# Modulation blocks in the array's quarters, filter directions on its row halves, and weight blocks loaded earlier

## The chip, the cores and the metric

The kernel runs on one core of one Trainium2 chip. A core has a matrix unit (TensorE, in the profile PE, with its weight loads as PEld), VectorE (DVE), ScalarE (ACT), GpSimd (POOL) and SyncE (SP), which here issues the DMA transfers. They work from their own queues, each in its own order, and wait for one another by semaphores. The metric is the device time of one execution in microseconds; less is better.

## The reference, cut to what matters

Two layers of a hybrid diffusion trunk run on 128 context tokens and 1024 latent tokens with the same weights. Each layer is RMSNorm, a shift and scale, a mixer, a gate, and a residual add; shift, scale and gate come from a conditioning vector (the "modulation").

```python
def ada_mod(cvec, w, b):
    m = jax.nn.silu(cvec) @ w + b
    shift, scale, gate = jnp.split(m, 3, axis=-1)
    return shift[:, None], scale[:, None], gate[:, None]
```

For layer l, w has shape (1024, 3072), and there are two conditioning vectors: one for the context, one for the latents. Layer 0's mixer has SSD heads and Hyena channels side by side, behind one projection of 1024 to 6688 columns; layer 1's is a neighbourhood attention. A Hyena channel is a long convolution whose filter comes from a small network of the token's position, once forward and once backward:

```python
    hdn = jnp.sin(freq * (feats @ w1 + b1))
    hdn = jnp.sin(freq * (hdn @ w2 + b2))
    filt = (hdn @ w3).astype(f32)
    decay = jnp.exp(-t * jnp.abs(deltas)[None])
    h_fwd = filt[:, :D_B] * decay
    h_bwd = filt[:, D_B:] * decay
```

The last step is `y = rms_norm(x + g * out)` on both streams.

## The kernel before, in words

Activations lie transposed: 128 of the 1024 features on the partitions, all 1152 tokens along the row, so eight tiles make one activation. Precise products are split in three: a tile or a weight block is cut into a high part (a cast by ScalarE, line 132 for weights) and the rest (a subtraction by VectorE, line 133), and TensorE does high x high, high x low and low x high. A projection (`proj`, lines 160 to 162) takes one block of weights of 1024 x 128, loops over three blocks of 384 tokens and eight feature tiles, and so issues 72 products. Weight blocks come in a fixed list; `w_next` splits the next one and loads the one after.

Beside these projections runs background work. `self.bg` is a list of generators; after each block of 384 tokens `tick` adds a rate to a credit and takes as many steps of the first generator as there is credit. The order in which the instructions then stand on each engine isn't that of the source: a planner lays it out from the dependencies, the order of the source as priority, and its own estimates of time. Tiles come from pools; tiles of one tag share as many buffers as the pool has, and a new one waits until the old one's last reader is done. PSUM, where products are summed, has two pools: three banks for projections (`pj`) and five for all else (`ps`, in the profile bg).

What the change touches, in the order of time:

- **Start** (`run`, from line 1413 on). x is loaded in eight tiles on SP's queue (at the end of `open`'s small loads and the filter network's), then the modulation blocks 0 and 1, the first weight block, modulation block 2, the second weight block, and more modulation blocks. ScalarE squares x, VectorE adds the eight squares (line 1484), TensorE sums them over the features (`token_sums`, line 347), and `rstd_rep` makes the norm factors of them: a power on GpSimd, three diagonal blocks on VectorE, three products (line 338), copies. `make_h` then makes the eight modulated tiles (lines 355 to 361), in step with the first two projections. In between, the filter network is fed step by step: `filter_mlp` yields after each piece, and `sin_layer` is its sine: five operations of VectorE and one of ScalarE, with a scratch tile `k` (tag "sq" in the start's own pool). The squares use the buffers hh6, hh7 and hh0 of the later activation in turn; the last one is in hh6.
- **Filters** (`filter_groups` and `filter_time`, in the background of the stage "xbc", rate 1.0). For each of eight groups of 128 channels `filter_time` makes the filter in time: nine blocks of 128 positions, three products each (lines 514 to 516), whose weights are the network's 128 rows (64 forward, 64 backward) and whose moving side is w3, laid out as a block-diagonal matrix of 128 x 256 with zeros written by GpSimd. Two blocks share a bank; ScalarE makes four decays (line 519, tile dc) and VectorE multiplies them in (line 520). Then come a Fourier stage on VectorE and TensorE and a store of the spectrum.
- **Modulation** (`ada_gen`, `ada_mm`, `ada_row`, `ada_cols`, in the background of the stage "z", rate 2.0). Sixteen blocks of 256 columns. For each, four products at a time stand side by side in the array's columns, 32 each (line 290): they take four different blocks of 128 rows of the weights, in two halves. So a bank holds four partial sums in four quarters of its partitions; a row copy takes it out (line 296), and two selecting products (line 306) add the four quarters up and turn the result to columns, to which VectorE adds the bias (line 309). For the last gate the rows go to DRAM (growd).
- **Final stage** (`final`). The gate of layer 1 is needed along the row here: growd's 128 rows are loaded, and four selecting products (line 1364) with the constant sel4b spread the sum to all partitions; VectorE adds the bias (line 1365). They stand behind the fifth of eight steps of the first six output blocks.

Of the kernel before, what the change touches and what calls it, by code (L numbers as in the profile page):

```python
# [9 lines left out]
AF = mybir.ActivationFunctionType  # L10
# [7 lines left out]
T = 1152  # L18
# [29 lines left out]
class Net:  # L48
# [147 lines left out]
    def open(self):  # L196
# [18 lines left out]
        self.sel4 = self.t(self.p_c, [128, 2], "sel4")  # L215
        self.dma(self.sel4, i["sel4"])
        d = self.p_d
        self.Hd = self.t(d, [8, 128, 20, 128], "Hd")
# [8 lines left out]
        self.x1d = self.t(d, [NCH, 128, 1024], "x1d")  # L227
        self.growd = self.t(d, [128, 1024], "growd")
        self.Cd = self.t(d, [3, 16, 16, 480], "Cd")
# [20 lines left out]

    def ada_gen(self, blocks, pool):

        self.silu_wide(pool)
        todo = [(l, nb, half) for l, nb in blocks for half in range(2)]
        raw = {}

        def load(i):
            if i < len(todo):
                raw[i] = self.t(pool, [128, 1024], "wa", bufs=6)
                l, nb, half = todo[i]  # L260
                self.dma(raw[i], self.i["wada"][l, nb, half])

        for i in range(4):
            load(i)
        yield
        last = None
        for i, (l, nb) in enumerate(blocks):
            load(2 * i + 4)
            load(2 * i + 5)
            p = self.ps()  # L270
            self.ada_mm(p, 0, raw.pop(2 * i))
            yield
            self.ada_mm(p, 1, raw.pop(2 * i + 1))
            if last:
                self.ada_cols(*last)
            last = l, nb, self.ada_row(l, nb, p, pool)
            yield
        self.ada_cols(*last)

# [13 lines left out]
    def ada_row(self, l, nb, p, pool):  # L293

        row = self.t(pool, [128, 256], "row", bufs=2)
        self.nc.scalar.copy(row, p[:, :256])
        if l == 1 and nb >= 8:
            self.store(self.growd[:, (nb - 8) * 256:(nb - 7) * 256], row)
        return row
# [66 lines left out]

    def sin_layer(self, arg, pool):

        nc = self.nc
        M = 1.5 * 2.0 ** 23  # L370
        k = self.t(pool, [128, T], "sq")[:, 0:1152]
        nc.vector.tensor_scalar(out=k, in0=arg, scalar1=1.0 / (2 * math.pi), scalar2=M, op0=ALU.mult, op1=ALU.add)
        nc.vector.tensor_scalar(out=k, in0=k, scalar1=-M, scalar2=None, op0=ALU.add)
        nc.vector.scalar_tensor_tensor(out=arg, in0=k, scalar=-6.28125, in1=arg, op0=ALU.mult, op1=ALU.add)
        nc.vector.scalar_tensor_tensor(out=arg, in0=k, scalar=-(2 * math.pi - 6.28125), in1=arg, op0=ALU.mult, op1=ALU.add)
        nc.vector.tensor_scalar(out=arg, in0=arg, scalar1=3.1415925, scalar2=-3.1415925, op0=ALU.min, op1=ALU.max)
        nc.scalar.activation(arg, arg, AF.Sin)

    def filter_mlp(self, keep, pool, px):
# [18 lines left out]
        yield  # L398
        self.sin_layer(a, px)
        yield  # L400
# [8 lines left out]
        yield  # L409
        self.sin_layer(b, px)  # L410
        yield
# [76 lines left out]
    def filter_time(self, g, pool):  # L488

        nc = self.nc  # L490
        i = self.i

        w3 = self.t(pool, [128, 256], "w3")
        wh = self.t(pool, [128, 256], "w3h", F32R)
        wl = self.t(pool, [128, 256], "w3l", F32R)
        nc.gpsimd.memset(w3[0:64, 128:256], 0.0)
        nc.gpsimd.memset(w3[64:128, 0:128], 0.0)
        for h in range(2):
            self.dma(w3[64 * h:64 * h + 64, 128 * h:128 * h + 128], i["hw3"][:, g, h])
# [3 lines left out]
        self.dma(dl.rearrange("p a c -> p (a c)"), i["dlhb"][g:g + 1].to_broadcast([128, 256]))  # L503
        F = self.t(pool, [128, 18, 128], "F", bufs=2)
        Fj = F[:, 0:16].rearrange("p (d j) c -> p j d c", d=2)
        hh, hl = self.hdn
        for j0 in range(0, 9, 2):
            n = min(2, 9 - j0)
            p = self.ps()
            dc = self.t(pool, [128, 2, 2, 128], "dc")  # L510
            for j in range(j0, j0 + n):
                o = p[:, (j - j0) * 256:(j - j0) * 256 + 256]
                js = slice(j * 128, j * 128 + 128)
                nc.tensor.matmul(o, hh[:, js], wh, start=True, stop=False)
                nc.tensor.matmul(o, hl[:, js], wh, start=False, stop=False)
                nc.tensor.matmul(o, hh[:, js], wl, start=False, stop=True)
                for d in range(2):
                    n1 = 8 * d + j if j < 8 else 16 + d
                    nc.scalar.activation(dc[:, j - j0, d], dl[:, 0], AF.Exp, scale=self.tcol[:, n1:n1 + 1])
            nc.vector.tensor_tensor(out=Fj[:, j0:j0 + 2] if n == 2 else F[:, 16:18].unsqueeze(1),  # L520
                                    in0=p[:, :n * 256].rearrange("p (j d c) -> p j d c", j=n, d=2), in1=dc[:, :n], op=ALU.mult)

        nc.vector.tensor_tensor(out=F[0:1, 0:17:16], in0=F[0:1, 0:17:16], in1=bc(dl[0:1, 1:2], [1, 2, 128]), op=ALU.add)
        return F

    def filter_groups(self, pool):
# [4 lines left out]
        self.dma(self.tcol, self.i["tcol"])  # L531
        Fn = self.filter_time(0, pool)
        yield
        for g in range(8):
            F = Fn
            sm = self.t(pool, [128, 8, 128], "sm")
# [4 lines left out]
            yield  # L541
            if g < 7:
                Fn = self.filter_time(g + 1, pool)
                yield
            H = self.t(pool, [128, 20, 128], "H")
# [791 lines left out]
    def final(self, pool, ys, ws):  # L1337
# [19 lines left out]
        for k in range(8):  # L1357
            for (c, b), p in first.items():
                mm(p, c, slice(b * 512, b * 512 + 512), k)
            if k == 4:  # L1360
                for s in range(2):
                    for b in range(2):
                        p = self.ps()
                        nc.tensor.matmul(p, sel4b[:, s, :], rows[:, b * 512:(b + 1) * 512], start=True, stop=True)
                        V.tensor_tensor(out=gr[:, s, b * 512:(b + 1) * 512], in0=p, in1=bg[:, b * 512:(b + 1) * 512], op=ALU.add)
        for c in range(NCH):
# [46 lines left out]
    def run(self, upto="end"):  # L1413
# [21 lines left out]
        with self.pool("x0") as px:  # L1435
# [6 lines left out]
            def load(n):  # L1442
# [11 lines left out]
                for half in range(2):  # L1454
                    self.dma(r[half], self.i["wada"][0, blocks[n], half])
                raws[n] = r
# [198 lines left out]
def host(x):  # L1655
# [10 lines left out]

    o["wada"] = con(x["w_ada"].reshape(2, 2, 4, 128, 12, 256).transpose(0, 4, 1, 3, 2, 5).reshape(2, 12, 2, 128, 1024))

# [58 lines left out]
def constants():  # L1727
# [10 lines left out]
    o["sel4"] = s4.reshape(128, 2)  # L1738
    o["sel4b"] = np.ascontiguousarray(np.repeat(o["sel4"][:, :, None], 128, 2))
    o["sel64"] = np.tile(np.eye(32, dtype=f), (2, 1))  # L1740
# [101 lines left out]
```

## Time and profile before

| | |
|---|---|
| three runs, us | 2075.86, 2077.14, 2079.71 |
| profiled execution, us | 2079.07, its span 2077.3 |
| granted TensorE clock of the profiled execution | 0.995 |
| moved by DMA | 257.13 MB, mean 124 GB/s |
| filter products (lines 514, 515, 516) | 72 each, 287, 281 and 281 ns |
| modulation products (line 290), all stages | 19.8 us busy in the z stage, 256 records |
| selecting products (line 306), z stage | 64 records, 253 ns |

How to read it: an instruction on single-precision numbers stands as two records, one on numbers that are cut to fewer bits (fp32r) as one. Matmuls are pipelined: a product of 384 columns lasts some 340 ns in the records, but the next one starts 0.17 us after it. So a group's busy time or mean says little of what it costs TensorE, and the distance from start to start says more. The rows of the order of time give: start, length, engine, line, operation, written and read tiles, shape, count, and in brackets the idle time before and what ended it.

### The profile page before, as it was taken

How to read it: one execution, taken by the hardware profiler on the slowest of the kernel's cores; microseconds unless marked ns; L12 is line 12 of the kernel's file. 1: busy time of each engine (PE TensorE's matmuls, PEld its weight loads, DVE VectorE, ACT ScalarE, POOL GpSimd, SP SyncE). 2: the span in 40 equal slices, each digit the busy share in tenths (PEclk: the TensorE clock that was granted, in tenths of full speed). 3: DMA queues.
4: the chain of work that ended last, by engine and by line, in shares of the span. 5: the costliest groups of instructions: out<-in, count | busy, mean ns of one | idle time of the engine just before them, and what ended most of it. 6: DMA issues, size and time to landing. Idle time of an engine off the chain costs nothing.

```text
span 2077.3 us, 33946 instructions
## 1 busy us (share of the span) xinstructions
PE 2019.4 (97%) x13088; PEld 1820.7 (88%) x13088; DVE 1313.7 (63%) x2720; ACT 917.9 (44%) x2100; POOL 110.5 (5%) x233
## 2 busy tenths in 40 slices
PE   5999999999999999999999999999999999999998
PEld 3999997889999999888888899998888888888877
DVE  6887745145778787898899774654444344454464
ACT  3676642263333322554466511535445454443232
POOL 0010001110000000000000000100000000000000
PEclk9999999999999999999999999999999999999999
DMA  8142349554222113433353351422333223333462
GB/s 340 47 150 93 107 166 295 206 181 163 80 74 72 65 58 102 152 120 127 117 180 109 129 167 41 120 81 86 95 115 88 78 79 97 111 117 123 129 212 82
DMA packets 114265, 257.13 MB, mean 124 GB/s; under 512 B 27031, under 2 KB 62487, under 8 KB 111639
## 3 DMA queue, kind: packets, MB, share of 16 engines
q1 hardware_dynamic: 98728, 191.87, 29.1%
q0 software_dynamic: 15376, 63.09, 8.3%
q8 instruction: 104, 1.70, 0.4%
q14 instruction: 57, 0.47, 0.1%
HBM read 187.10 MB, written 67.80 MB: 123 GB/s over the span
## 4 chain that ended last, share of the span: by engine, by line
PE 82%; DVE 7%; DMA 4%; ACT 3%; issue 3%; SPq 0%; POOL 0%; POOLq 0%; DVEq 0%; ACTq 0%
PE pj L160 15%; PE pj L161 15%; PE pj L162 15%; PE bg L1315 3%; PE bg L1327 3%; PE bg L1298 3%; PE pj L1155 2%; PE pj L1156 2%; PE pj L1157 2%; PE bg L778 1%; PE bg L777 1%; PE bg L915 1%; PE pj L1353 1%; PE bg L290 1%; PE pj L1354 1%
## 5 line engine op out<-in xcount | busy, mean ns | idle before, releaser
L160 PE MATMUL pj<-hh,whi 128*128 128x384 f32 x1728 | 601.1, 348 | 2.7 <-DVE acc L846 1.8
L161 PE MATMUL pj<-hl,whi 128*128 128x384 f32 x1728 | 586.4, 339 | 0.0
L162 PE MATMUL pj<-hh,wlo 128*128 128x384 f32 x1728 | 586.1, 340 | 0.0
L160 PEld LDWEIGHTS pj<-hh,whi 128*128 128x128 f32 x1728 | 324.7, 188 | 23.7 <-issue 18.0
L161 PEld LDWEIGHTS pj<-hl,whi 128*128 128x128 f32 x1728 | 324.9, 188 | 7.5 <-issue 6.6
L162 PEld LDWEIGHTS pj<-hh,wlo 128*128 128x128 f32 x1728 | 324.6, 188 | 5.5 <-issue 4.5
L133 DVE TENSOR_TENSOR wlo<-wraw,whi 128x1024 fp32r<-128x1024 f32 x108 | 131.7, 1221 | 156.0 <-ACT whi L132 153.3
L132 ACT CAST whi<-wraw 128x1024 fp32r<-128x1024 f32 x108 | 113.3, 1050 | 259.1 <-PE pj L161 229.6
L1233 DVE CUSTOM_DVE_ANT_0 sz<-bg,Tb 128x512 f32<-128x512 f32 x128 | 83.5, 688 | 127.3 <-PE bg L1298 126.7
L583 ACT COPY raw<-pj 128x384 f32<-128x384 f32 (+2 forms) x140 | 56.0, 402 | 171.2 <-PE pj L162 84.0
L1235 ACT ACTIVATE sz<-sz,mx 128x512 f32<-128x512 f32 x128 | 91.6, 717 | 54.0 <-DVE mx L1233 53.2
L160 PE MATMUL pj<-yhi,whi 128*128 128x384 f32 x324 | 111.4, 344 | 3.8 <-DVE x L1076 2.8
L162 PE MATMUL pj<-yhi,wlo 128*128 128x384 f32 x324 | 110.8, 342 | 0.0
L161 PE MATMUL pj<-ylo,whi 128*128 128x384 f32 x324 | 109.7, 339 | 0.0
L1329 ACT COPY Pt<-bg 128x512 f32<-128x512 f32 (+1 forms) x144 | 71.9, 548 | 32.1 <-PE bg L1327 28.3
L1155 PE MATMUL pj<-whi,hh 128*128 128x256 f32 x288 | 82.9, 289 | 0.0
L1156 PE MATMUL pj<-wlo,hh 128*128 128x256 f32 x288 | 80.8, 281 | 0.0
L1157 PE MATMUL pj<-whi,hl 128*128 128x256 f32 x288 | 80.5, 280 | 0.0
L1327 PE MATMUL bg<-csq,sz 128*128 128x128 f32 x528 | 73.9, 280 | 0.0
L908 ACT ACTIVATE xw<-xt,wd 128x64 f32<-128x64 f32 x256 | 64.6, 336 | 8.7 <-PE bg L915 8.1
L1327 PEld LDWEIGHTS bg<-csq,sz 128*128 128x128 f32 x528 | 56.7, 141 | 13.0 <-issue 12.7
L160 PEld LDWEIGHTS pj<-yhi,whi 128*128 128x128 f32 x324 | 61.4, 189 | 7.1 <-issue 5.5
(411 smaller groups left out, 4021.3 us busy)
## 6 DMA issues: line engine op xcount, KB each, us to landing
wraw<-in_we SPq DMA_DIRECT2D x52, 512.0 KB, 3.6
wa<-in_wada SPq DMA_DIRECT2D x32, 512.0 KB, 6.8
wraw<-in_wo SPq DMA_DIRECT2D x24, 512.0 KB, 3.6
Tb<-Cd SPq DMA_DIRECT2D x256, 48.0 KB, 2.0
Hd<-H POOLq DMA_DIRECT2D x8, 1280.0 KB, 5.4
H<-Hd SPq DMA_DIRECT2D x8, 1280.0 KB, 6.5
xt<-xtd SPq DMA_DIRECT2D x17, 512.0 KB, 4.5
wraw<-in_woe SPq DMA_DIRECT2D x16, 512.0 KB, 4.2
```

Source lines behind the costliest of these rows:

```text
L132: self.nc.scalar.copy(hi, r)
L133: self.nc.vector.tensor_tensor(out=lo, in0=r, in1=hi.bitcast(F32), op=ALU.subtract)
L160: nc.tensor.matmul(p[:, :NB], wh, xh[k][:, sl], start=(k == 0), stop=False)
L161: nc.tensor.matmul(p[:, :NB], wh, xl[k][:, sl], start=False, stop=False)
L162: nc.tensor.matmul(p[:, :NB], wl, xh[k][:, sl], start=False, stop=(k == nk - 1))
L1155: nc.tensor.matmul(p[:, :256], self.hh[k][:, ts], hi[:, q:q + 256], start=(k == 0), stop=False)
L1156: nc.tensor.matmul(p[:, :256], self.hh[k][:, ts], lo[:, q:q + 256], start=False, stop=False)
L1157: nc.tensor.matmul(p[:, :256], self.hl[k][:, ts], hi[:, q:q + 256], start=False, stop=(k == 7))
L1233: V.tensor_tensor_reduce(out=z[:, :n], in0=s, in1=tb, scale=-1.0, scalar=3.0e38, op0=ALU.add, op1=ALU.min, accum_out=m1)
L1235: nc.scalar.activation(z[:, :n], z[:, :n], AF.Exp, bias=m1, scale=-1.0, accum_out=sm)
L1327: nc.tensor.transpose(pt[:, b * 128:(b + 1) * 128], p[:, b * 128:(b + 1) * 128], self.ident)
L1329: nc.scalar.copy(t[:, :nb * 128], pt[:, :nb * 128])
```

## The change

Four things are done.

1. *Start.* The first two weight blocks are loaded directly after x, ahead of all modulation blocks. The first sine layer takes its scratch from the buffer hh6, the second as before. A small constant (sel8) is loaded behind sel4.
2. *Filters.* `filter_time` makes two groups at a time. w3's two halves of 64 rows hold the forward and the backward weights of both groups side by side, without zeros; every product takes 64 rows, forward on the upper half of the array and backward on the lower, each into its own bank. The decays and the evacuation go by group and direction. It is called four times in place of eight, for the next pair behind the first part of the odd group's spectrum. The bias row hb takes w3's buffer.
3. *Modulation.* In the z stage four groups of 1024 columns take the place of sixteen blocks of 256. The four quarters of the array now hold the same block of 128 rows of the conditioning vectors, and each takes another 256 columns of the weights; eight steps add up in one bank. The result stands as it is, with no partial sums. Two selecting products with sel8 (8 columns) serve a whole group. The start's eight blocks stay as they were.
4. *Final stage.* growd is only 2 rows. They are loaded to all partitions, and VectorE adds the bias; the selecting products and sel4b go.

The diff, cut to its core:

```diff
-    def ada_gen(self, blocks, pool):
+    def ada_gen(self, groups, pool):
...
-        todo = [(l, nb, half) for l, nb in blocks for half in range(2)]
+        todo = [(n, k) for n in range(len(groups)) for k in range(8)]
...
+        def cols(l, a, row):
+            q = self.ps()
+            for j in range(2):
+                nc.tensor.matmul(q[:, 8 * j:8 * j + 8], row[:, j * 128:(j + 1) * 128], self.sel8, start=True, stop=True)
+            m = self.mod[l][0][:, a]
...
         last = None
-        for i, (l, nb) in enumerate(blocks):
-            load(2 * i + 4)
-            load(2 * i + 5)
-            p = self.ps()
-            self.ada_mm(p, 0, raw.pop(2 * i))
+        for i, (n, k) in enumerate(todo):
+            load(i + 4)
+            if k == 0:
+                p = self.ps()
+            w = raw.pop(i)
+            for b in range(4):
+                nc.tensor.matmul(p[32 * b:32 * b + 32, :256], self.cs[:, k, :], w[:, b * 256:(b + 1) * 256],
+                                 start=(k == 0), stop=(k == 7))
+            if k == 1 and last:
+                cols(*last)
+            if k == 7:
+                l, a = groups[n]
+                row = self.t(pool, [128, 256], "row", bufs=2)
+                nc.scalar.copy(row, p[:, :256])
+                if (l, a) == (1, 2):
+                    for b in range(4):
+                        self.store(self.growd[:, b * 256:(b + 1) * 256], row[32 * b:32 * b + 2, :])
+                last = l, a, row
             yield
...
-        self.sin_layer(a, px)
+
+        self.sin_layer(a, self.t(self.p_h, [128, T], "hh6")[:, 0:1152])
...
-        self.sin_layer(b, px)
+        self.sin_layer(b, self.t(px, [128, T], "sq")[:, 0:1152])
...
-        w3 = self.t(pool, [128, 256], "w3")
+        w3 = self.t(pool, [128, 2, 128], "w3")
...
-        nc.gpsimd.memset(w3[0:64, 128:256], 0.0)
-        nc.gpsimd.memset(w3[64:128, 0:128], 0.0)
         for h in range(2):
-            self.dma(w3[64 * h:64 * h + 64, 128 * h:128 * h + 128], i["hw3"][:, g, h])
+            self.dma(w3[64 * h:64 * h + 64], i["hw3"][:, g:g + 2, h])
...
+        hb = self.t(pool, [128, 2, 128], "w3")
+        for m in range(2):
+            self.dma(dl[:, m], i["dlhb"][g + m:g + m + 1, 0:128].to_broadcast([128, 128]))
+            self.dma(hb[0:1, m], i["dlhb"][g + m:g + m + 1, 128:256])
+        Fs = [self.t(pool, [128, 18, 128], "F", bufs=2) for n in range(2)]
...
+            ps = [self.ps(), self.ps()]
             for j in range(j0, j0 + n):
...
+                for x, w, st, sp in ((hh, wh, True, False), (hl, wh, False, False), (hh, wl, False, True)):
+                    for r, p in zip(R, ps):
+                        nc.tensor.matmul(p[:, o], x[r, js], w[r], start=st, stop=sp)
+            for m, F in enumerate(Fs):
+                dc = self.t(pool, [128, 2, 2, 128], "dc")
+                for d, p in enumerate(ps):
+                    n1 = 8 * d + j0 if j0 < 8 else 16 + d
+                    for j in range(n):
+                        nc.scalar.activation(dc[:, d, j], dl[:, m], AF.Exp, scale=self.tcol[:, n1 + j:n1 + j + 1])
+                    nc.vector.tensor_tensor(out=F[:, n1:n1 + n], in0=p[:, :n * 256].rearrange("p (j g c) -> p g j c", j=n, g=2)[:, m],
+                                            in1=dc[:, d, :n], op=ALU.mult)
...
-            if g < 7:
-                Fn = self.filter_time(g + 1, pool)
-                yield
...
+            if g in (1, 3, 5):
+                Fs = self.filter_time(g + 1, pool)
+                yield
...
-        sel4b = self.t(pool, [128, 2, 128], "sel4b", bufs=1)
-        self.dma(sel4b, self.i["sel4b"])
-        rows = self.t(pool, [128, 1024], "x1t")
-        self.dma(rows, self.growd)
+        for s in range(2):
+            self.dma(gr[:, s], self.growd[s:s + 1].to_broadcast([128, 1024]))
+            V.tensor_tensor(out=gr[:, s], in0=gr[:, s], in1=bg, op=ALU.add)
...
-            if k == 4:
-                for s in range(2):
-                    for b in range(2):
-                        p = self.ps()
-                        nc.tensor.matmul(p, sel4b[:, s, :], rows[:, b * 512:(b + 1) * 512], start=True, stop=True)
-                        V.tensor_tensor(out=gr[:, s, b * 512:(b + 1) * 512], in0=p, in1=bg[:, b * 512:(b + 1) * 512], op=ALU.add)
...
-            load(0)
-            load(1)
             self.w_load(0)
-            load(2)
             self.w_load(1)
-            for n in (3, 4, 5, 7):
+            for n in (0, 1, 2, 3, 4, 5, 7):
                 load(n)
...
-        self.bg.append(self.ada_gen([(0, nb) for nb in range(8, 12)] + [(1, nb) for nb in range(12)], p_ad))
+        self.bg.append(self.ada_gen([(0, 2), (1, 0), (1, 1), (1, 2)], p_ad))
```

More of the change, by code (lines that the diff above doesn't have):

```diff
@@ L216, in open @@
         self.dma(self.sel4, i["sel4"])
+        self.sel8 = self.t(self.p_c, [128, 8], "sel8")
+        self.dma(self.sel8, i["sel8"])
         d = self.p_d
@@ L227, in open @@
         self.x1d = self.t(d, [NCH, 128, 1024], "x1d")
[L228 removed]
+        self.growd = self.t(d, [2, 1024], "growd")
         self.Cd = self.t(d, [3, 16, 16, 480], "Cd")
@@ L259, in load @@
                 raw[i] = self.t(pool, [128, 1024], "wa", bufs=6)
-                l, nb, half = todo[i]
-                self.dma(raw[i], self.i["wada"][l, nb, half])
+                n, k = todo[i]
+                self.dma(raw[i], self.i["wadg"][n, k])
+        def cols(l, a, row):
[3 more added lines that the diff above has]
+            m = self.mod[l][0][:, a]
+            o = PV[f"ba{l}"] + 8 * a
+            ba = self.pv[:, o:o + 8].rearrange("p (b j) -> p j b", j=2)
+            for j in range(2):
+                V.tensor_tensor(out=m.rearrange("p (b j) s -> p j b s", j=2)[:, j],
+                                in0=q[:, 8 * j:8 * j + 8].rearrange("p (b s) -> p b s", s=2),
+                                in1=bc(ba[:, j].unsqueeze(2), [128, 4, 2]), op=ALU.add)
+            if a == 1:
+                o = PV[f"nw{l}"]
+                V.scalar_tensor_tensor(out=m, in0=m, scalar=1.0, in1=bc(self.pv[:, o:o + 8].unsqueeze(2), [128, 8, 2]),
+                                       op0=ALU.add, op1=ALU.mult)
         for i in range(4):
@@ L266, in ada_gen @@
         last = None
-        for i, (l, nb) in enumerate(blocks):
-            load(2 * i + 4)
-            load(2 * i + 5)
-            p = self.ps()
-            self.ada_mm(p, 0, raw.pop(2 * i))
-            yield
[L273 to L276, printed above, removed]
-            yield
-        self.ada_cols(*last)
+        for i, (n, k) in enumerate(todo):
[16 more added lines that the diff above has]
+                last = l, a, row
+            yield
+        cols(*last)
     def ada_block(self, nb, raw, pool):
@@ L296, in ada_row @@
         self.nc.scalar.copy(row, p[:, :256])
-        if l == 1 and nb >= 8:
-            self.store(self.growd[:, (nb - 8) * 256:(nb - 7) * 256], row)
         return row
@@ L364, in make_h, with sin_layer @@
         self.hl.append(lo)
-    def sin_layer(self, arg, pool):
+    def sin_layer(self, arg, k):
         nc = self.nc
         M = 1.5 * 2.0 ** 23
-        k = self.t(pool, [128, T], "sq")[:, 0:1152]
         nc.vector.tensor_scalar(out=k, in0=arg, scalar1=1.0 / (2 * math.pi), scalar2=M, op0=ALU.mult, op1=ALU.add)
@@ L506, in filter_time @@
+        Fs = [self.t(pool, [128, 18, 128], "F", bufs=2) for n in range(2)]
         hh, hl = self.hdn
+        R = (slice(0, 64), slice(64, 128))
         for j0 in range(0, 9, 2):
             n = min(2, 9 - j0)
-            p = self.ps()
-            dc = self.t(pool, [128, 2, 2, 128], "dc")
+            ps = [self.ps(), self.ps()]
             for j in range(j0, j0 + n):
-                o = p[:, (j - j0) * 256:(j - j0) * 256 + 256]
                 js = slice(j * 128, j * 128 + 128)
[L514 to L524, printed above, removed]
+                o = slice((j - j0) * 256, (j - j0) * 256 + 256)
+                for x, w, st, sp in ((hh, wh, True, False), (hl, wh, False, False), (hh, wl, False, True)):
+                    for r, p in zip(R, ps):
+                        nc.tensor.matmul(p[:, o], x[r, js], w[r], start=st, stop=sp)
@@ L526, in filter_groups @@
+        for m, F in enumerate(Fs):
+            nc.vector.tensor_tensor(out=F[0:1, 0:17:16], in0=F[0:1, 0:17:16], in1=bc(hb[0:1, m:m + 1], [1, 2, 128]), op=ALU.add)
+        return Fs
     def filter_groups(self, pool):
@@ L531, in filter_groups @@
         self.dma(self.tcol, self.i["tcol"])
-        Fn = self.filter_time(0, pool)
+        Fs = self.filter_time(0, pool)
         yield
         for g in range(8):
-            F = Fn
+            F = Fs[g % 2]
             sm = self.t(pool, [128, 8, 128], "sm")
@@ L1454, in load @@
                 for half in range(2):
-                    self.dma(r[half], self.i["wada"][0, blocks[n], half])
+                    self.dma(r[half], self.i["wada"][blocks[n], half])
                 raws[n] = r
@@ L1738, in constants @@
     o["sel4"] = s4.reshape(128, 2)
-    o["sel4b"] = np.ascontiguousarray(np.repeat(o["sel4"][:, :, None], 128, 2))
+    s8 = np.zeros((4, 32, 4, 2), f)
+    for b in range(4):
+        s8[b, 0, b, 0] = s8[b, 1, b, 1] = 1
+    o["sel8"] = s8.reshape(128, 8)
     o["sel64"] = np.tile(np.eye(32, dtype=f), (2, 1))
```

12 lines of the change are left out of this document (6 added, 6 removed).

## The prediction

> **What bounds the kernel now.** I read the page first, then the time of each stretch, then the order of instructions in the four places that the change touches.
>
> ```profile
> span 2077.3 us, 33946 instructions
> ...
> PE 2019.4 (97%) x13088; PEld 1820.7 (88%) x13088; DVE 1313.7 (63%) x2720; ACT 917.9 (44%) x2100; POOL 110.5 (5%) x233
> ...
> PE 82%; DVE 7%; DMA 4%; ACT 3%; issue 3%; SPq 0%; POOL 0%; POOLq 0%; DVEq 0%; ACTq 0%
> ```
>
> TensorE is busy 97% of the span and holds 82% of the chain that ended last. So a microsecond taken off TensorE's own stream is worth a microsecond, except in the places where another engine ends last. There are two of these among the stretches concerned (start:end, then for each engine its busy time and instruction count):
>
> ```profile
> 13.78:27.73 13.95, 0.00 (x0) 0.00 (x0) 13.69 (x12) 8.69 (x8) 0.00 (x0) 1.00 1.03 412
> 27.73:39.14 11.41, 11.40 (x62) 8.29 (x63) 3.20 (x9) 2.17 (x4) 1.83 (x1) 1.00 1.03 410
> 39.14:78.35 39.21, 37.72 (x273) 30.33 (x272) 35.00 (x54) 21.38 (x37) 0.40 (x2) 1.00 0.31 114
> 82.00:150.00 68.00, 65.47 (x477) 62.34 (x476) 63.06 (x125) 50.73 (x141) 11.35 (x27) 1.00 0.37 125
> ```
>
> In the first 14 us shown TensorE does nothing and VectorE is full (13.69 of 13.95): VectorE decides. From 39 to 150 us both are nearly full (35.00 of 39.21, then 63.06 of 68.00).
>
> Busy time hides overlap, so below I take TensorE's cost from start to start: the distance from an instruction to the next.
>
> **1. The start: sine layer and loads.** All rows are from the order of instructions but two, a group of VectorE and a group of DMA issues.
>
> ```profile
> 1.65 0.42 SPq L86 DMA_DIRECT2D sel<-in_sel  x1
> ...
> 10.17 4.62 SPq L86 DMA_DIRECT2D hh<-in_wada  x4
> 10.18 1.16 ACT L1482 ACTIVATE xacc<-hl 128x1152 f32<-128x1152 f32 x1 [5.14 <-DMA hl<-in_xT]
> ...
> 14.47 1.16 ACT L1482 ACTIVATE hh<-hl 128x1152 f32<-128x1152 f32 x1 [0.27 <-DMA hl<-in_xT]
> ...
> 15.89 0.33 SPq L86 DMA_DIRECT2D wraw<-in_we  x1
> ...
> 27.74 4.00 PE L347 MATMUL bg<-csq,xacc 128*128 128x1 f32 x18 [14.72 <-DVE xacc L1484]
> ...
> 36.37 1.23 DVE L133 TENSOR_TENSOR wlo<-wraw,whi 128x1024 fp32r<-128x1024 f32 x1
> ...
> 39.14 0.35 DVE L355 SCALAR_TENSOR_TENSOR hh<-hl,mod,xacc 128x128 f32<-128x128 f32 x1 [1.28 <-ACT xacc L341]
> ...
> 43.53 1.22 DVE L133 TENSOR_TENSOR wlo<-wraw,whi 128x1024 fp32r<-128x1024 f32 x1
> ```
>
> ```profile
> L1484 DVE TENSOR_TENSOR xacc<-xacc,hh 128x1152 f32<-128x1152 f32 x7 | 9.5, 1353 | 0.2
> ...
> hh<-in_wada SPq DMA_DIRECT2D x4, 512.0 KB, 11.1
> ```
>
> The token sums wait until 27.74 for seven adds. These cost 9.5 us of the 13.95; the other 4.4 us are the sine layer, which VectorE puts between them. The changed sine layer keeps its scratch in hh6, the buffer that also holds the square that the last add reads. So it cannot begin before that add: a wait is added, and the adds get VectorE for themselves. Then the arrival of x is their limit: four squares from 10.18 to 14.47 are 1.43 us apart, the eighth starts at 10.18 + 7 x 1.43 = 20.2 and ends at 21.4, its add at 22.7. That is 5.0 us before 27.74. Against it: the new load of sel8 stands ahead of x on SP's queue (0.42 by the row of sel, so 0.4 is taken), and the sine layer's 4.4 us fall on VectorE just when the row sums come back, 4.0 us after the token sums start; up to 0.8 us of it is in the way. What is queued behind the sine layer on VectorE, the diagonal blocks and splits, has had room: 3.20 us busy of 11.41 from 27.7 to 39.1. Result: 3.8 us earlier.
>
> The first two weight blocks move ahead of two modulation blocks on SP's queue. Their subtractions (1.23 and 1.22) now stand at 36.37 and 43.53, in the path to and inside the full stretch from 39 us; they can go into the gap before. I take 1.0 of the 2.45. The modulation blocks moved back by two loads of 1.43 us: the fourth half is issued at about 14.8 + 2.9 + 0.4 = 18.1 instead of under 14.8 and lands 11.1 later, at 29.2. Its products, the second half of the modulation work that follows the token sums, are wanted at about 29. So this is even, and costs perhaps 0.3. Term: **-4.5**. Ends: -6.5 (adds 5.0 and subtractions 2.4, less 0.9), and -1 if the full stretch 39 to 78 us does not move up with its start.
>
> **2. Filter directions on row halves.** The first two rows are the ends of a run of 27 filter products; then a run of score products in the attention, the nearest thing to the new form (64 rows, two at a time).
>
> ```profile
> 160.69 0.28 PE L514 MATMUL bg<-w3h,hdh 128*128 128x256 f32 x1
> ...
> 163.89 0.34 PE L160 MATMUL pj<-hh,whi 128*128 128x384 f32 x1
> ```
>
> ```profile
> 1508.91 0.28 PE L1157 MATMUL pj<-whi,hl 128*128 128x256 f32 x1
> 1509.12 0.50 PE L1298 MATMUL bg<-KH,QH 64*128 64x512 f32 x2
> 1509.46 0.40 PE L1298 MATMUL bg<-KL,QH 64*128 64x512 f32 x2
> 1509.70 0.40 PE L1298 MATMUL bg<-KH,QL 64*128 64x512 f32 x2
> 1510.02 0.39 PE L1155 MATMUL pj<-whi,hh 128*128 128x256 f32 x1
> 1510.25 0.28 PE L1156 MATMUL pj<-wlo,hh 128*128 128x256 f32 x1
> ```
>
> 27 products take 3.20 us, 0.1185 each; 8 groups x 27 = 216 make 25.6 us. After it there are 4 pairs x 9 x 6 = 216 again, of half the rows. Two score products of 512 columns start together and the next two 0.24 later, which is one product's time at this rate (512/256 x 0.1185 = 0.237). So 108 couples, 12.8 us. But a change between whole array and halves costs: 0.21 instead of 0.12 on entry, 0.34 and 0.32 instead of 0.24 for the first and last couple, 0.23 instead of 0.12 after it: 0.38 us for each run. The Trainium skill, TensorEngine Tiling (Array Packing), section Key Properties, says that changing the tiling mode drains TensorE; the trace agrees, at these 0.38 us.
>
> How many runs there will be I cannot see: 4 if each pair's 54 stand together, more where banks run out. A pair's 18 blocks need ten banks, two at a time, of a pool of five, and each couple of banks is read by two channel groups before it is free. With about four runs in each pair, 16 x 0.38 = 6.1; 12.8 + 6.1 = 18.9, against 25.6. Term: **-6.5**. Ends: 4 runs give -11.3; couples that never overlap give 25.6 + 6.1, +6.1.
>
> The evacuation grows. Groups of VectorE and ScalarE:
>
> ```profile
> L520 DVE TENSOR_TENSOR F<-bg,dc 128x512 f32<-128x512 f32 x32 | 21.9, 685 | 17.5 <-PE bg L516 8.7 <-ACT dc L519 8.6
> ...
> L520 DVE TENSOR_TENSOR F<-bg,dc 128x256 f32<-128x256 f32 x8 | 3.4, 421 | 4.1 <-ACT dc L519 4.1
> ```
>
> ```profile
> L519 ACT ACTIVATE dc<-dl,tcol 128x128 f32<-128x128 f32 x144 | 46.9, 395 | 22.9 <-DMA dl<-in_dlhb 11.4 <-DVE F L520 11.4
> ```
>
> Now 32 x 0.685 + 8 x 0.421 = 25.3 us; then 80 pieces of 256 elements or fewer, at most 80 x 0.421 = 33.7. So up to 8 us more VectorE, of which about 2 us come back because half of the weight splits and hidden waits go. The 144 exponentials stay, still on one buffer dc. From 82 to 150 us VectorE has 4.9 us left, and the first pairs put four filters there early, so I take **+2.5** (ends 0 and +8, all of it on the path). The added wait: the bias row hb uses w3's buffer, so its load stands on SP until the subtraction for w3l is done, and the second decay load and the next projection weights stand behind it. The weights are fetched one block (three steps of some 8 us) ahead; I cost it at nothing, inside the +8. The two clears on POOL go; nobody on the path waited for POOL.
>
> **3. Modulation in quarters.** One tick of the z stage, and a place with two steps together:
>
> ```profile
> 367.85 0.64 PE L290 MATMUL bg<-wa,cw 128*32 128x256 f32 x8
> 368.42 0.61 PE L306 MATMUL bg<-sel,row 128*128 128x2 f32 x4
> 368.96 0.64 PE L290 MATMUL bg<-wa,cw 128*32 128x256 f32 x8
> 369.53 0.44 PE L160 MATMUL pj<-hh,whi 128*128 128x384 f32 x1
> ```
>
> ```profile
> 319.29 1.07 PE L290 MATMUL bg<-wa,cw 128*32 128x256 f32 x16
> 320.29 0.44 PE L160 MATMUL pj<-hh,whi 128*128 128x384 f32 x1
> ```
>
> The products (256 records) already run in quarters and stay; what goes are 12 of 16 selections. Now a block costs 1.68 us (367.85 to 369.53), 16 of them 26.9. Then 12 ticks of 1.00 without a selection and 4 of 1.00 + 0.54 make 18.2: -8.7. Some selections stand already between full runs, so I take **-8**. Ends: 12 x 0.54 = -6.5, and -9. Loads stay 32 of 512 KB. The accumulator bank is held for eight steps in place of two, out of five; nothing else of weight uses that pool there. Row copies (ScalarE) and sums (VectorE) fall from 16 to 4; both have room, so no gain.
>
> **4. The final stage.**
>
> ```profile
> 1994.41 3.79 PE L1364 MATMUL bg<-x1t,sel4b 128*128 128x512 f32 x8
> 1997.63 0.80 PE L1352 MATMUL pj<-whi,yhi 128*128 128x512 f32 x1
> ```
>
> The gate selection goes: 1994.41 to 1997.63, **-3.2**. Two broadcast loads and two adds on VectorE replace it. If these loads come late, the adds hold up VectorE's splits behind them; loads of this size landed within 11.1 us above, and the gate is read some 12 us after SP issues them. Ends -3.2 and +2.
>
> **Sum** against the profiled execution (2079.07, that is span 2077.3 and 1.8 around it): -4.5 - 6.5 + 2.5 - 8 - 3.2 = -19.7, 2059.4. This execution is 1.9 above the median of the runs, 2077.14, so the forecast is 2057.4.
>
> **The rivals.**
> - *Evacuation sets the pace of the filter stage.* The banks are freed by ScalarE and VectorE, which nearly fill 82 to 150 us; TensorE's 6.5 us turn into waits and VectorE adds 4 us: -11.7, time 2065.5. For: 63.06 of 68.00. Against: TensorE shows only 2.5 us idle there, and the filters' work is spread over twelve projections, not this stretch alone. The Trainium skill's same page, section PSUM Bottleneck, says that tiling speeds up TensorE but not the evacuation; no run here shows yet which it is.
> - *The start does not move.* The stretch from 39 us is nearly full on two engines, and if a modulation block lands late its start is held: term -1, time 2061.
> - *The halves do not overlap* (it doesn't do what it says): +6.1 for -6.5, time 2070. Against: the score products.
> - *Slower: TensorE stands at the banks.* If a pair's 54 products stand in one run on TensorE, as 27 do now, the third block of each pair waits for a bank. One round is four exponentials (4 x 0.395) and two products (0.84), 2.4 us; a bank pair needs two rounds, 4.8; three such releases less some 2 us of products are 12 us a pair, 48 us for four: -19.7 + 48, time 2105. It decides from 5 us of such waits a pair (20 / 4). Against: at present the planned order puts projection products between filter products when banks are short.
>
> **How the numbers follow.** Forecast 0.56 (2057.4), evacuation 0.19, start 0.12, no overlap 0.06, standing at banks 0.07. A measurement here tells about 0.2%, 4.2 us, from no change. The first three and half of the fourth lie beyond it, less a twentieth of their weight for bad ends together: faster 0.86, same 0.07, slower 0.07. Range: the best ends of start, filter, z and final together would give -30; I go to -31, 2046. Above, evacuation at its end (+8) and no overlap reach about -6, 2071.
>
> **What would show it.** Token sums near 23 us and the first make_h near 35; filter products starting in twos about 0.12 apart; in the z stage runs of 16 with four selections; no TensorE work between the last first-block products and the main loop of the final stage. Wrong if TensorE's idle time from 80 to 290 us grows by over 5 us, or if a filter product waits for F.

## The result and the profile after

| | before | after |
|---|---|---|
| median, us | 2077.42 (4 runs, 2075.86 to 2079.71) | 2100.04 (4 runs, 2096.6 to 2104.47) |
| ratio after/before | | 1.0101, 95% interval 1.0084 to 1.0119 |
| profiled execution, us | 2079.07 | 2104.47 (slowest of the four) |

The change makes the kernel 1% slower. First the page of the changed kernel: span, busy times, chain.

```profile
span 2102.7 us, 33796 instructions
...
PE 2027.0 (96%) x13032; PEld 1824.3 (87%) x13032; DVE 1315.1 (63%) x2743; ACT 914.1 (43%) x2084; POOL 108.1 (5%) x217
...
PE 61%; issue 23%; DVE 8%; DMA 4%; ACT 3%; POOL 1%; SPq 0%; POOLq 0%; DVEq 0%; ACTq 0%
```

TensorE does 56 fewer instructions and is busy 7.6 us longer; "issue" grew from 3% to 23%. Neither line says where. For that I cut both traces at the same work: at the 1st, 241st, 385th, 1513th and last of the 2052 products of line 160 (24 make a weight block), and at the end of the last product of all. The time of each stretch of before (start:end, length, then busy time by engine, granted clock, DMA share and GB/s):

```profile
0.00:82.22 82.22, 57.09 (x371) 43.71 (x372) 56.17 (x86) 39.84 (x60) 3.02 (x13) 1.00 0.58 222
82.22:308.80 226.58, 224.05 (x1577) 218.84 (x1576) 167.75 (x325) 141.74 (x377) 23.93 (x57) 1.00 0.35 123
308.80:430.10 121.30, 120.73 (x844) 100.55 (x844) 40.18 (x81) 31.72 (x71) 14.84 (x23) 1.00 0.70 229
430.10:1318.96 888.86, 877.42 (x5114) 807.96 (x5113) 694.95 (x1445) 371.09 (x865) 32.53 (x87) 1.00 0.34 113
1318.96:1960.99 642.03, 633.32 (x4722) 564.81 (x4722) 286.85 (x671) 297.26 (x666) 30.50 (x44) 0.99 0.35 103
1960.99:2070.15 109.16, 106.77 (x468) 84.79 (x467) 65.91 (x112) 35.00 (x60) 5.12 (x8) 0.98 0.43 149
```

and of after:

```profile
0.00:82.99 82.99, 56.75 (x364) 41.98 (x364) 55.37 (x84) 38.36 (x55) 2.67 (x9) 0.96 0.58 220
82.99:331.71 248.72, 234.44 (x1583) 222.61 (x1582) 173.75 (x367) 143.92 (x379) 22.95 (x49) 0.95 0.38 125
331.71:453.24 121.53, 117.57 (x796) 98.03 (x796) 36.01 (x65) 27.07 (x58) 13.56 (x20) 0.96 0.58 195
453.24:1343.10 889.86, 876.99 (x5115) 808.05 (x5113) 695.42 (x1445) 371.50 (x865) 32.65 (x87) 1.00 0.34 113
1343.10:1990.13 647.03, 637.89 (x4723) 569.80 (x4722) 287.39 (x671) 297.02 (x666) 30.60 (x44) 0.99 0.35 102
1990.13:2095.90 105.77, 103.38 (x460) 83.88 (x459) 65.19 (x110) 35.02 (x60) 5.13 (x8) 0.98 0.45 157
```

Length against length: start +0.8, filter stage +22.1, z stage +0.2, then +1.0, attention +5.0, final stage -3.4: together +25.7; the span grew by 25.4. The filter stage is nearly the whole loss. Idle time in it is length less busy: 2.5 before, 14.3 after, **+11.8**. The granted clock fell from 1.00 to 0.95. Before has no half-clock stretch here, after has four:

```profile
107.12:113.94 6.82, 5.58 (x17) 5.58 (x18) 6.82 (x17) 5.37 (x14) 1.25 (x3) 0.50 0.39 127
141.25:151.49 10.24, 8.19 (x38) 7.41 (x39) 5.66 (x16) 5.16 (x18) 0.00 (x0) 0.50 0.23 68
206.10:209.52 3.42, 3.42 (x17) 3.08 (x17) 3.42 (x13) 0.85 (x4) 1.01 (x1) 0.50 0.33 96
233.41:236.82 3.41, 3.41 (x12) 2.97 (x11) 1.57 (x5) 2.56 (x8) 0.00 (x0) 0.50 0.00 0
```

In these 23.9 us TensorE is busy 20.6. If a product takes twice as long at half the clock, half of the 20.6 is loss: **+10.3**. What is left, busy less that, I call the products' own time: 224.05 before, 234.44 - 10.3 = 224.1 after, so **no change**. The waits of TensorE in this stretch of after (total, times, longest), then of before:

```profile
PE bg L543 <- DVE F L550: 4.9, 4, 2.6
PE bg L576 <- ACT raw L728: 3.0, 1, 3.0
PE pj L160 <- ACT acc L615: 1.9, 1, 1.9
PE bg L503 <- DVE F L550: 1.9, 1, 1.9
PE bg L497 <- DVE A L469: 1.8, 1, 1.8
```

```profile
PE bg L679 <- DVE F L520: 0.8, 1, 0.8
PE bg L471 <- ACT acc L680: 0.6, 1, 0.6
PE pj L160 <- ACT acc L584: 0.6, 1, 0.6
```

Filter products (L543) now wait for banks that the multiply by the decay (L550) has yet to free, and what is queued behind them waits too. The order of time of after, in the first pair and, in the last row, in the second:

```profile
91.07 0.28 PE L543 MATMUL bg<-w3h,hdl 64*128 64x256 f32 x1
91.19 0.28 PE L543 MATMUL bg<-w3l,hdh 64*128 64x256 f32 x1
...
97.52 0.28 PE L543 MATMUL bg<-w3h,hdl 64*128 64x256 f32 x2
...
97.64 0.28 PE L543 MATMUL bg<-w3l,hdh 64*128 64x256 f32 x2
...
104.84 0.40 DVE L554 TENSOR_TENSOR F<-F,w 1x256 f32<-1x256 f32 x1
...
105.34 0.68 PE L576 MATMUL bg<-F,tcf 128*128 128x128 f32 x4 [2.98 <-ACT raw L728]
...
106.44 0.47 DVE L550 TENSOR_TENSOR F<-bg,dc 128x128 f32<-128x128 f32 x2
...
107.17 1.21 DVE L568 TENSOR_TENSOR sm<-F 128x1024 f32<-128x1024 f32 x1
...
141.42 0.55 PE L543 MATMUL bg<-w3h,hdh 64*128 64x256 f32 x1 [2.56 <-DVE F L550]
```

Where two halves have work at once, they do what they should: two products start together, 0.12 after the two before (97.52, 97.64). But often one half works alone (91.07, 91.19). Counted over all 216 filter products of after, 58 couples start within 0.02 us of each other, of 108 that were possible.

The pair's last multiply is at 106.44, 8.8 us after the last couple, among other work of ScalarE and VectorE, and VectorE's part of the Fourier stage of the first group begins only then (107.17). TensorE stands 2.98 us before that group's first Fourier products (L576). The view names ScalarE's L728, but that ended at 104.92. These products read F, and VectorE added F's bias row until 105.24 (L554), 0.1 before they start: the wait is for the first group's filter, not for a bank. A wait for a bank is the one of 2.56 in the second pair (141.42).

### The profile page after: what moved, and what is told of

Its sections match the earlier page's. It is cut to its first block, busy times and chain, and to the rows that moved or that the text cites. A ratio compares the mean times of both kernels' runs of the same rounds, so it can differ in the third digit from the quotient of the medians.

```text
span 2102.7 us, 33796 instructions
## 1 busy us (share of the span) xinstructions
PE 2027.0 (96%) x13032; PEld 1824.3 (87%) x13032; DVE 1315.1 (63%) x2743; ACT 914.1 (43%) x2084; POOL 108.1 (5%) x217
## 4 chain that ended last, share of the span: by engine, by line
PE 61%; issue 23%; DVE 8%; DMA 4%; ACT 3%; POOL 1%; SPq 0%; POOLq 0%; DVEq 0%; ACTq 0%
PE pj L160 12%; PE pj L161 12%; PE pj L162 11%; PE bg L809 1%; PE bg L808 1%; PE pj L1384 1%; PE pj L1382 1%; PE pj L1383 1%; PE bg L503 1%; PE bg L946 1%; PE bg L504 1%; PE bg L505 1%; PE bg L506 1%; PE bg L1021 1%; PE bg L1055 1%
```

## The experiments

Theories at the outset. **T1**: each bank is read by two groups in two rounds of evacuation and so comes free late. **T2**: the row halves themselves cost TensorE (mode changes, products that don't overlap). **T3**: the altered start leaves the filter stage a backlog.

**mod_final**: start and filter functions of before, all else as after.

> The kernel before with the modulation quarters and the final stage of the change; the start and the filter stage are those of before. T1 (each bank's evacuation is split between two channel groups and frees the banks late), T2 (row halves cost TensorE itself) and T3 (the altered start leaves a backlog) all say the same of it: -8 to -11 us, so 2066 to 2070 us. Over 2075 would mean that the loss is in the modulation and that all three are wrong.

2076.85 us, ratio 0.9985 (0.9967 to 1.0003): unclear, and less than every theory said. It is over the 2075 that were to mean that the loss is in the modulation; filter_only below shows that it isn't. What was wrong is the gain that all three theories took for granted. See mod_final_pad.

**start_only**: before, with the two weight loads ahead of the modulation's and the sine's scratch in hh6.

> The kernel before with the new start alone: first weight blocks loaded ahead of the modulation's, the sine layer with a scratch of its own. T1 and T2: 2075 to 2081 us, since token sums come 3 us sooner but the row copy on ScalarE stands behind the sine. T3 (the start leaves the filter stage a backlog): 2090 us or more.

2081.97 us beside 2080.6 of before on that chip, ratio 0.9994 (0.9976 to 1.0012). No gain and no harm: T3 falls, and so does the start term.

**filter_only**: before, with `filter_time` and `filter_groups` of after.

> The kernel before with the new filter layer and filter groups alone. T1 and T2: the whole loss of the filter stage without the gains elsewhere, 2097 to 2111 us, with granted clock at half in several stretches between 83 and 350 us. T3: 2071 to 2083 us.

2105.43 us, ratio 1.0113 (1.0086 to 1.0141). The whole loss is in these two functions. Its row of the stretch from the 1st to the 241st product:

```profile
81.90:327.17 245.27, 230.44 (x1584) 218.53 (x1583) 173.69 (x367) 143.62 (x379) 23.32 (x49) 0.97 0.39 127
```

Idle is 14.8, against 14.3 in after.

**merged_evac**: one round frees a bank.

```diff
-for m, F in enumerate(Fs):
-    dc = self.t(pool, [128, 2, 2, 128], "dc")
-    for d, p in enumerate(ps):
+for d, p in enumerate(ps):
+    dc = self.t(pool, [128, 2, 2, 128], "dc")
+    for m in range(2):
         # exponentials for group m, direction d
-        nc.vector.tensor_tensor(F of group m, 256 elements)
+    nc.vector.tensor_tensor(F2 of both groups, 512 elements)
```

> The changed kernel, filter products still on row halves two groups at a time, but both groups' filters stand in one tile, so that a bank (one direction, two groups) is freed by one round: four exponentials of 128 elements and one multiply of 512, in place of two rounds on the one decay buffer. T1: the waits of TensorE for the banks from 83 to 345 us and most half-clock stretches go, 2060 to 2072 us. T2: as after, 2094 to 2106 us. T3: 2085 us or more.

2099.94 us, ratio 1.0082 (1.0054 to 1.011), no better than after (1.0101; the intervals overlap). TensorE is idle 14.4 us in the stretch (246.32 less 231.94): T1 falls. What merged_evac left as it was is the amount: a pair takes ten banks, two at a time, from a pool of five, in one step of the background work. Before, a group takes exactly five, and by the trace its 27 products waited for the multiply 0.4 us in all, over all eight groups. That became **T4**. **T5**, its rival: the one decay buffer makes ScalarE and VectorE take turns, and that sets the pace.

**split_pair**: a pair in three steps.

```diff
 for j0 in range(0, 9, 2):
     ...
+    if j0 in (2, 6):
+        yield
```

> The changed kernel, with the filter layer of a pair of groups given out in three steps in place of one: two couples of blocks (four banks), two couples, the last block, each a step of the background work, so that projection work stands between them. T4 (a pair asks for ten banks of five in one step; TensorE stands until ScalarE and VectorE have freed them, and the work behind it stands too): waits of TensorE from 83 to 345 us fall from 18 to under 8 us, half clock in that stretch from about 28 us to under 10, time 2070 to 2085 us. T2 (the row halves themselves cost TensorE): no change against the changed kernel, 2095 us or more. T5 (the single decay buffer sets the pace of the evacuation, wherever the products stand): 2092 us or more.

2090.91 us, ratio 1.006 (1.0039 to 1.0082). T2 and T5 said 2095 and 2092 or more, which four runs from 2088 to 2097 don't rule out; T4 was right in direction and too bold in size. The stretch, and TensorE's largest waits in it:

```profile
84.90:320.01 235.11, 225.56 (x1584) 215.02 (x1582) 173.74 (x361) 144.78 (x378) 21.06 (x44) 0.98 0.30 101
```

```profile
PE bg L577 <- ACT raw L729: 3.0, 1, 3.0
PE bg L543 <- ACT H L581: 2.1, 1, 2.1
PE pj L160 <- ACT acc L616: 1.9, 1, 1.9
...
PE bg L543 <- DVE F L550: 0.6, 2, 0.3
```

The waits of filter products for the multiply fell from 4.9 to 0.6, idle to 9.6, and the stretch is 13.6 us shorter than in after. What stays is the wait of 3.0 for the first group's filter and its consequence.

**dc_halves**: a decay buffer for each multiply.

```diff
-dc = self.t(pool, [128, 2, 2, 128], "dc")
 for d, p in enumerate(ps):
+    dc = self.t(pool, [128, 2, 128], "dc", bufs=2)
```

> The changed kernel with the one decay buffer cut into two half-sized ones, one for each multiply, so that the exponentials of the next multiply need not wait for the last. T5 (that hand-over between ScalarE and VectorE paces the release of banks): 2075 to 2088 us, ScalarE's waits for the multiply fall from 10 us to under 3. T4: 2093 to 2104 us, since the other work in both queues and the ten banks at once remain. T2: 2095 us or more.

2099.08 us, ratio 1.0089 (1.0068 to 1.011): T5 falls. ScalarE's waits for the multiply did fall, from 10.2 to 5.6 us and not to under 3, and the time didn't follow.

**merged_split** (both edits, and the sine layer after the row sums):

> All remedies together: three steps for a pair, one round of evacuation for a bank (four exponentials, one multiply of 512), and in the start the sine layer after the row sums. T4: the best of the forms with row halves, 2058 to 2072 us. T2: 2090 us or more.

2095.59 us, ratio 1.0085 (1.0065 to 1.0104): a miss for T4 as well, by 24 us, and in T2's range. TensorE is idle 9.5 us in the stretch, as in split_pair, so the merged round and the sine layer bring nothing that can be seen beside it (1.006).

**mod_final_sine** (start and rest of after, filters of before, sine after the row sums):

> The change without its filter stage (that of before), with the sine layer given out after the row sums. The modulation quarters, the final stage and the loads ahead stay. If the start's 3 us sooner token sums reach the projections once the sine layer is out of their way: 2069 to 2074 us; if not, as with the modulation and final stage alone, 2075 to 2079 us.

2079.0 us, ratio 1.0004 (0.9991 to 1.0017): the start isn't cured by that order. But the order didn't get the sine out of the way either: TensorE still waits 5.39 us for the modulation's row copy, and the first make_h is at 41.03.

**full_rows**: after with pairs, banks, order and evacuation as they are, but every product over the whole array. The weights of a pair are 512 wide, with zeros in the other direction's rows:

```diff
-R = (slice(0, 64), slice(64, 128))
+R = (slice(0, 256), slice(256, 512))
...
-nc.tensor.matmul(p[:, o], x[r, js], w[r], start=st, stop=sp)
+nc.tensor.matmul(p[:, o], x[:, js], w[:, r], start=st, stop=sp)
```

> The changed kernel with its pairs, its banks, its order and its evacuation, but each filter product over the whole array: the weights of the other direction are zeros, so no product is on a row half and no change of mode occurs. Left out: the bias row of the filters, and the decay of a pair's first group serves both. T4 (ten banks of five in one step): as slow as the changed kernel or some 5 us slower, 2095 to 2110 us, idle and half clock from 82 to 330 us as there. T2 (row halves cost TensorE): 2072 to 2088 us.

2098.22 us, ratio 1.0087 (1.0068 to 1.0107). The stretch:

```profile
82.51:324.38 241.87, 230.83 (x1584) 224.57 (x1583) 172.92 (x359) 144.48 (x379) 25.14 (x55) 0.97 0.39 128
```

No row half is left, and most of the loss is: the stretch is 15.3 us longer than before's, against 22.1 in after (idle 11.0, clock 0.97). T2 falls: the pairs cost most of the time, not the halves. One thing more differs: the raw weights of a pair stand in the decay buffer here, which ties their load to the multiplies; what that costs isn't known.

**first_single**: split_pair, with groups 0 and 1 made one by one by the old function (**T6**: what is left is that group 0 has to wait for two groups' filters).

> The form with three steps for a pair, and the first two groups made one by one as before, over the whole array; pairs on row halves from the third group. T6 (what three steps left is the first pair: group 0 waits for both groups' filters in the fullest stretch): 2076 to 2086 us, TensorE idle between first projection block and block 10 (82 to 310 us) from 9.6 us to under 6. If the rest comes from pairs anywhere: 2088 us or more.

2083.61 us, ratio 1.0024 (1.0012 to 1.0036): T6 holds in time. But not in idle:

```profile
82.66:312.74 230.08, 220.44 (x1578) 212.74 (x1577) 168.93 (x349) 141.09 (x373) 21.72 (x45) 0.99 0.31 106
```

Idle is 9.6 still, against under 6 expected. The clock is nearly whole, and the stretch is 5.0 us shorter than in split_pair.

**mod_final_pad**: mod_final with the selection table sel8 loaded where the modulation begins, its tile padded to 64 bytes.

> Modulation quarters and final stage alone, as once before, with the small selection table loaded at the modulation's own start rather than ahead of x, and its tile padded from 32 to 64 bytes, so that the buffers behind it keep their old alignment. If its load cost the start 2.8 us and the shift of addresses the attention 3 to 5 us: 2069 to 2074 us; if only the load: 2073 to 2077; if neither: 2076 to 2079 us.

2072.68 us, ratio 0.9967 (0.9955 to 0.998): **faster than before, by 0.33%**. Start and z stage:

```profile
0.00:80.50 80.50, 55.17 (x371) 42.49 (x371) 56.16 (x86) 39.81 (x60) 3.03 (x13) 1.00 0.60 226
...
307.36:422.51 115.15, 114.56 (x796) 96.13 (x796) 38.28 (x70) 27.27 (x59) 14.74 (x23) 0.99 0.71 236
```

and the start of mod_final, where the table is loaded ahead of x:

```profile
0.00:84.96 84.96, 59.81 (x370) 45.71 (x371) 56.28 (x86) 39.90 (x60) 3.02 (x13) 0.98 0.57 215
```

The start is 4.5 us shorter with the load out of x's way, 1.7 of it clock (0.02 x 85). Not all of this is the load: the token sums come only 0.34 sooner (28.25 to 27.91), and best and best_32, with the same start, take 82.57 and 82.18. The time lies in the range for both guesses together, but by luck: the attention stays 5 us longer than before (646.92 to 642.03), so the padding isn't what it wanted. Nor is the step from mod_final to mod_final_pad itself clear of noise, as the two intervals overlap.

**best** and **best_32**: start of before, table late, final stage and modulation of after, groups 0 and 1 singly, pairs in three steps; best_32 has 32 background steps as before, best 35.

> The start of before, the modulation quarters with that table late and padded, the final stage, the first two groups one by one and later pairs on row halves in three steps. By T4 and T6 the halves then save TensorE's stream 2 to 4 us and the rest as in the modulation and final stage alone: 2066 to 2076 us. If pairs still leave waits: 2080 us or more.

> As the composite run before (start of before, modulation quarters with the table late and padded, final stage, first two groups one by one, later pairs on row halves in three steps), without the empty step behind each pair, so that the filter work has 32 steps, as many as before, in place of 35. If the halves pay and the composite lost it because three steps came after the projections that cover them: 8 us come back at the end of the filter stage (block 10, before at 308.8 us), time 2065 to 2073 us, at or below the 2072.7 of modulation and final stage alone. If pairs cost what the halves save: 2074 to 2081 us.

2079.98 us, 1.0007 (0.9997 to 1.0018), and 2079.54 us, 0.9997 (0.9986 to 1.0007). best lies between its two ranges, best_32 in the one for pairs that cost what the halves save. The stretch of best_32:

```profile
82.18:312.61 230.43, 222.29 (x1578) 213.92 (x1577) 169.43 (x352) 141.68 (x374) 21.65 (x45) 0.99 0.35 120
```

The clock is at half for 6.83 us of it, all of them busy, so 3.4 are lost. Own time is 222.29 - 3.4 = 218.9, 5.2 less than before: this much the halves save TensorE in three pairs, where 62 of 81 possible couples start together. Idle is 8.1, 5.6 more than before, and 3.4 go to the clock. What the halves save, waits and clock take; the best kernel here leaves the filter stage alone.

## Why the prediction was wrong

Forecast 2057.4, range to 2071; measured 2100.04. From the 2059.4 forecast for the profiled execution to the 2104.47 measured, 26.1 us are the filter stage (-4.0 forecast, +22.1 measured), 8.2 the z stage, 5.3 the start, and 6.0 the two stretches behind the z stage, for which the sum had no term. The upper end was also added up wrong: evacuation at +8 and no overlap make -19.7 + 5.5 + 12.6 = -1.6, some 2075 and not 2071. The measured time is beyond either.

- **Filter row halves (-6.5): overlap right, size not.** Couples do start 0.12 apart, but the sum took all 216 products as 108 couples in some 16 runs. In after 58 couples start together, in 20 runs. At the sum's own prices this wins 58 x 0.1185 = 6.9 us and loses 20 x 0.38 = 7.6 (an estimate from its rows), and own time didn't change. With 62 of 81 couples in 10 runs, in best_32, it fell by 5.2.
- **Evacuation (+2.5, "ends 0 and +8, all of it on the path"): the step that failed.** It counted VectorE's longer multiplies as the cost. VectorE's busy time did rise by 6.0 in the stretch (167.75 to 173.75), but the cost is TensorE's: +11.8 of waits and 10.3 of work at half clock, a term that the sum didn't have at all. That the loss lies in the filter functions is shown (filter_only), and that it comes with pairs and mostly not with halves (full_rows). How the pairs bring it is shown in part. A pair in three steps brings the ratio from 1.0101 to 1.006, and the first two groups singly to 1.0024; this fits a step that asks for ten banks of five, and a first group that waits for two groups' filters, but the two weren't separated, and merged_split came out worse than T4 says. The prediction had the numbers in hand ("A pair's 18 blocks need ten banks, two at a time, of a pool of five"). Another suspect falls by the trace: a pair takes both buffers of F, but in after the multiplies (L550) wait only for decays (17.1 us) and filter products (0.7), never for a reader of F.
- **The rival "TensorE stands at the banks" (0.07, 2105)** named the mechanism and nearly the time. It was waved off by "the planned order puts projection products between filter products when banks are short". That held only in part: a pair is one step. Its price was composed otherwise than told: 11.8 us of waits in all, not 48, of them 4.9 for banks that the multiply frees, and 10.3 from the clock. The 19.7 us of gains that it took off didn't come, so that its time is near the measured one is luck. Both signs of being wrong came true: TensorE's idle time from 80 to 290 us grew from 2.5 to 14.3, and filter products wait for the multiply that writes F.
- **Start (-4.5, ends -6.5 and -1): outside its ends**, +0.8 in after and -0.2 in start_only. After loses 2.4 to half clock (35.44 to 42.27 us, 4.83 of them busy), start_only nothing. The token sums did come earlier (24.64 for 27.74, where the prediction had them near 23). But the prediction followed the sine layer on VectorE alone. The order of time of after:

```profile
24.64 1.01 PE L373 MATMUL bg<-csq,xacc 128*128 128x1 f32 x4 [10.82 <-DVE xacc L1505]
...
35.96 1.16 ACT L402 ACTIVATE H<-H 128x1152 f32<-128x1152 f32 x1 [3.72 <-DVE H L401]
...
37.03 0.35 ACT L324 COPY row<-bg 128x256 f32<-128x256 f32 x1
...
37.44 1.01 PE L332 MATMUL bg<-sel,row 128*128 128x2 f32 x4 [4.64 <-ACT row L324]
...
40.48 0.35 DVE L381 SCALAR_TENSOR_TENSOR hh<-hl,mod,xacc 128x128 f32<-128x128 f32 x1 [1.64 <-ACT xacc L367]
```

The sine (L402) waits on ScalarE for VectorE's last piece; the modulation's row copy (L324) stands behind it in ScalarE's queue, TensorE waits 4.64 for that copy, and the first make_h is at 40.48, later than the 39.14 of before. In start_only the same wait is 4.13 and the first make_h at 39.71. That nothing else would then have held the start isn't shown, since no run has the row copy ahead of the sine.
- **Modulation quarters (-8): size right in TensorE's own time, lost in place.** The clock is at half for 10.24 us of the z stage in after, with TensorE busy 9.41 of them. So own time is 120.73 before and 117.57 - 4.7 = 112.9 after: -7.9. In after, 4.0 of idle and the 4.7 of clock ate it; in mod_final_pad, without the pairs, these are 0.6 and 1.7 (3.41 us at half clock), and the stretch is 6.2 shorter (121.30 to 115.15).
- **Final stage (-3.2): right**, -3.4 (109.16 to 105.77).
- **sel8's load**, priced at 0.4 inside the start: with the load late the token sums come 0.34 sooner (28.25 in mod_final, 27.91 in mod_final_pad). What it costs the start beyond that isn't shown.
- **Open**: the attention is 5 us longer in after (642.03 to 647.03) and 4.9 in mod_final_pad, with equal counts; in filter_only and start_only, without the new modulation and final stage, it is 2.0 and 1.1, and these two are at half clock there for 6.8 and 3.4 us more than before, which after and mod_final_pad are not. Which of the two brings it, and how, wasn't tried.

## What to carry to other kernels

Before making two of something at once, count the buffers that one step asks for against the pool: for five of five the filter products waited 0.4 us, for ten of five 4.9, and with what waited behind them and the clock the stretch grew by 22 us. On TensorE, where it is nearly always busy, waits had a second price here, 10.3 us of half clock beside 11.8 of waits; charge both. And when a step is moved, follow each of its instructions on its own engine's queue, with what then stands behind it.

## What the hardware showed unexpectedly

A half-clock stretch can follow waits of under 2 us. The time of stretches of after:

```profile
202.60:206.10 3.50, 1.67 (x11) 1.34 (x10) 1.34 (x6) 2.60 (x6) 0.00 (x0) 1.00 0.03 8
206.10:209.50 3.40, 3.40 (x16) 3.06 (x16) 3.40 (x13) 0.85 (x4) 1.01 (x1) 0.50 0.33 96
209.50:212.90 3.40, 3.40 (x29) 3.40 (x28) 1.90 (x4) 1.24 (x5) 0.00 (x0) 1.00 0.26 77
```

TensorE was busy 1.67 of 3.50 us, the longest wait being 1.8 us, and then ran 3.40 us at 0.50, fully busy, before the clock came back. And of dc_halves, where a stretch that is 32% busy (1.05 of 3.30) is followed by 17.10 us at half clock, with TensorE 79% busy on average:

```profile
117.50:120.80 3.30, 1.05 (x18) 0.85 (x16) 3.30 (x12) 0.00 (x0) 0.08 (x1) 0.99 0.83 348
120.80:137.90 17.10, 13.46 (x59) 11.86 (x60) 12.70 (x31) 13.70 (x43) 1.55 (x3) 0.50 0.23 76
137.90:141.00 3.10, 3.10 (x30) 3.09 (x29) 3.07 (x5) 2.02 (x6) 0.00 (x0) 1.00 0.21 61
```

The Trainium skill, TensorE: Matmul & The Clock Gate, Part 1: The HAM clock gate, says that TensorE's clock falls to half after an idle window of about 3.4 us and returns after a busy one. The lengths agree (3.40, and 17.10 is five times that); but no window here was idle through, and one that was busy 1.67 of 3.50 us came right before the half clock. A fixed busy share doesn't explain it either: in dc_halves two windows in a row with 1.64 of 3.41 us busy (332.41 to 339.24) were followed by the full clock, and in after one that was busy throughout (366.53 to 369.94, in part with small products) by 3.42 us at half. Cut into five windows, the 17.10 us are busy 1.68, 2.42, 2.45, 3.42 and 3.41 us: the clock came back behind the second full window, not the first. What share of a window counts isn't known from these runs.
